# Experts' places as bfloat16 products, transposed feed-forwards and paired mLSTM heads in a two-block transformer kernel

## The chip, the cores and the metric

The kernel runs as one program on one core of a Trainium2 chip. The metric is the device time of one execution in microseconds (us); of several runs the median is given. Beside the times there is one execution recorded by the hardware profiler.

## The reference

Input is one sequence of 256 tokens by 1024 features in float32. Two blocks follow each other.

The first block adds two terms to x. One is attention: RMS norm, projection to q, k, v, four differential heads and eight plain heads, an output projection. The other is a mixture of 32 experts (four groups of eight): each token picks a group, then its two best experts in it, and `silu(t @ w_gate[e]) * (t @ w_up[e]) @ w_down[e]` of both is added with the router's weights.

The second block has four steps, each with its own RMS norm:

```python
x = x + 0.5 * swiglu(rms(x), w_gate, w_up, w_down)        # ffn1, hidden width 2816
z = rms(x) @ w_in + b_in                                  # split into q, k, v, conv inputs, gates
y_attn  = sliding_window_attention(a_q, a_k, a_v, sinks) @ w_proj_attn      # 16 heads, 4 kv heads, window 128
y_mlstm = (sigmoid(m_o) * rms(mlstm(m_q, m_k, m_v, m_i, m_f))) @ w_proj_mlstm  # 8 heads
x = x + (g0 * y_attn + g1 * y_mlstm) @ w_out              # this step is called mix below
x = x + 0.5 * swiglu(rms(x), ...)                         # ffn2, then a last RMS norm
```

## The kernel before

**Stages.** In order of time: attention of the first block (to about 141 us), experts (to about 341), ffn1 (to about 541), mix (to about 805) and ffn2 with the last norm.

**Dense products.** Float32 weights come as units of 128 x 1536 elements (768 KB) over SyncE's DMA queue (L104) into a ring of buffers. A unit is cut into pieces of 128 x 512, and each piece is split in two: ScalarE writes the rounded `hi` (L123), VectorE the rest `lo` (L132). Activations are split alike into `xh` and `xl`. Each product is then three TensorE passes (`mm3`: hi by xh, lo by xh, hi by xl), all issued by the helper `mm` (L207, in the changed kernel L220). There are two forms. `dense_tok` keeps 128 tokens stationary and streams 512 weight columns, so tokens end up on partitions. `dense_T` keeps a 128 x 128 piece of weights stationary and streams all 256 tokens, so features end up on partitions.

**Side work.** A `Side` object holds jobs (Python generators) that are advanced by `pump()`, which is called after each contraction step of a dense product; `yield 3` means three pumps later. TensorE and the other engines execute in the order in which the program issues, so the pumps fix where a small job's matmuls stand between the large ones.

**Feed-forward.** The hidden width 2816 is worked in 11 chunks of 256. For each chunk `dense_tok` makes gate and up side by side in two PSUM tiles (one for each half of the tokens), 48 matmuls of 512 columns. Then `hidden` runs as a side job: ScalarE takes silu of gate with the token's norm factor r as scale (L1297), VectorE multiplies by up and r (L1298), three pumps later TensorE transposes h in four small matmuls (L262), and h is split into `hh` and `hl` (L1304, L1305). The down product of the chunk before (24 matmuls) stands between one chunk's gate and up and the next's. r comes from GpSimd's Newton steps (L247 to L253).

**Experts.** Tokens are routed to 11 groups of four experts with 32 places each. P (256 tokens x 128 places, zeros and ones) is a group's placing matrix. The gather job collects x through P in two PSUM tiles of tag t, evacuated piece by piece by ScalarE (L1012) and VectorE (L1010) in turn; then two matmuls with P give the places' weights (`wsl`, L1022), and two transposes of P (L1025) the matrix PT for the way back. PSUM has two buffers of tag t and two of tag b.

**Mix.** For each of eight mLSTM heads a matmul with `pick` spreads the head's running maximum M over partitions (M holds 40 rows, L1410 and after), two matmuls make scores from 64 rows of q and k, and three more use them with the values. `window_job` does the window attention for two heads at a time, each with 64 rows of its own.

Of the kernel before, what the change touches and what calls it, by code (L numbers as in the profile page):

```python
# [10 lines left out]
F32 = mybir.dt.float32  # L11
# [8 lines left out]
D = 1024  # L20
# [27 lines left out]
class Stream:  # L48
# [31 lines left out]
    def early(self, first, pool, tag, bufs):  # L80

        self.open(pool, tag, bufs, self.k.stop)
        for i in range(first, first + bufs):
            self.fetch(i, self.pools[-1])
# [110 lines left out]

class Kernel:
# [68 lines left out]
    def new_xt(self):  # L265
        self.xt = (self.xp.tile([128, 8, S], F32R, name="xh", tag="xh"),
                   self.xp.tile([128, 8, S], F32R, name="xl", tag="xl"))
# [130 lines left out]
    def dense_T(self, acc, xt, cts=4, first=0):  # L398

        for kk in range(first, 8):  # L400
# [25 lines left out]
    def build(self):  # L426
# [29 lines left out]
        self.xn = self.xp.tile([128, 2, D], F32, name="xn")  # L456
# [29 lines left out]
    def qk_norm(self, at, acc, gcol, heads, name, then=None):  # L486
# [9 lines left out]
        if name == "qd":  # L496
            self.rB, self.rB2 = (at.tile([128, S], F32, name=f"rB{q}") for q in range(2))
# [6 lines left out]
        dst = heads[name] = at.tile([128, 4, S], F32, name=name, tag={"km": "qd"}.get(name, name))  # L504
# [163 lines left out]
    def attention1(self):  # L668
# [3 lines left out]
        with ExitStack() as es:  # L672
# [3 lines left out]
            self.new_xt()  # L676
            heads["y"] = y = self.xt
# [8 lines left out]
        y = [p[:, 4:] for p in y]  # L686
# [32 lines left out]
        self.st.open(self.xp, "xn", 1, self.stop)  # L719
        self.st.add_pool(self.xp, "xl", 1, self.last - 8)  # L720
# [10 lines left out]
    def diff_out(self, at, v, wT, heads):  # L731
# [5 lines left out]
        for h in range(4):  # L737
            p = self.pt([128, S], "b")
            c = slice(h * 128, (h + 1) * 128)
            self.mm(p, v[:, 0, c], wT[h][:, 0:256], True, False)  # L740
            self.mm(p[:, 128:256], v[:, 1, c], wT[h][:, 256:384], False, True)
# [20 lines left out]
    def moba_out(self, v, wT, y, j):  # L762
        nc = self.nc
        p = self.pt([128, S], "b")
        for hf in range(2):
# [3 lines left out]
            self.mm(p[o], v[:, 0, c], w[:, 0:256], True, False)  # L769
            self.mm(p[o, 128:256], v[:, 1, c], w[:, 256:384], False, True)  # L770
        nc.scalar.activation(y[0][:, 4 + j], p, AF.Copy)
        nc.vector.tensor_sub(y[1][:, 4 + j], p, y[0][:, 4 + j].bitcast(F32))

    def attention1_in(self, at):
# [41 lines left out]
        for n in range(2):  # L816
            acc = [self.pt([128, 512], "a") for tt in range(2)]
            self.dense_tok(acc, lambda kk: (xt[0], xt[1], kk))
            t = self.xn[:, n].rearrange("p (t n) -> p t n", t=2)
            nc.scalar.activation(t[:, 0], acc[0], AF.Copy, scale=self.r[:, 0:1])  # L820
            if n == 0:
                nc.scalar.activation(t[:, 1], acc[1], AF.Copy, scale=self.r[:, 1:2])
            else:
                nc.vector.tensor_scalar(t[:, 1], acc[1], self.r[:, 1:2], None, op0=OP.mult)
# [10 lines left out]
    def route_open(self):  # L835
# [6 lines left out]
        cb = bp.tile([128, 322], F32, name="cb")  # L842
        nc.scalar.dma_start(cb, self.i["cb"])
        self.iota, self.idx, self.e3 = (cb[:, a:b] for a, b in ((128, 256), (256, 289), (289, 322)))
        self.ones, self.before = (bp.tile([128, 128], BF16, name=f"m{q}") for q in range(2))
        nc.gpsimd.memset(self.ones, 1.0)
        nc.gpsimd.tensor_copy(self.before, cb[:, 0:128])
# [4 lines left out]
        self.le = [bp.tile([128, 4, 8], F32, name=f"le{tt}") for tt in two]  # L852
        self.oh = [[bp.tile([128, 33], BF16, name=f"oh{tt}{j}") for j in two] for tt in two]
        self.hT = self.xn.rearrange("p t (k n) -> p (t k) n", n=S)
# [38 lines left out]
    def select(self):  # L893
# [12 lines left out]
        key = bp.tile([128, 33], F32, name="key")  # L906
        km = bp.tile([128, NG], F32, name="km")
        self.eq = eq = bp.tile([128, NG, 3], F32, name="eq")
        pe = bp.tile([128, 2, NG, 3], F32, name="pe")
# [25 lines left out]
    def weigh(self):  # L935
# [46 lines left out]
        self.gov = bp.tile([128, 2, NG, 3], F32, name="gov")  # L982
# [305 lines left out]
    def hidden(self, fp, c, gu, hT, wait=False):  # L1288
# [4 lines left out]
        if c == 0 and wait:  # L1293
            yield 4
# [568 lines left out]
```

## Time and profile before

| | |
|---|---|
| time, median of 3 runs | 1005.68 us (1005.47 to 1006.81) |
| profiled execution | 1005.48 us, of which 1003.7 us are the span of the profile |
| TensorE busy | 986.8 us (98% of the span), granted clock at its upper level nearly throughout |
| VectorE, ScalarE, GpSimd busy | 560.8, 505.3, 50.3 us |
| DMA | 235.29 MB, 234 GB/s on average, above 410 GB/s in most of the expert stage |

A busy time is summed over an engine's instructions; the ends of matmuls are modelled, so the distance between two starts tells more about the price of a matmul than its listed duration. The chain of waits is followed back from the last instruction and says at each step what ended last.

### The profile page before, as it was taken

Reading aid. Unit: us, or ns where it says so; the run is one execution under the profiler, and the core shown is the slowest. Engines: PE = TensorE matmul, PEld = TensorE weight load, DVE = VectorE, ACT = ScalarE, POOL = GpSimd, SP = SyncE. Lnnn points to the kernel's source line nnn. Section 1 sums busy time; section 2 is a strip of 40 time slices with the busy share of each in tenths; the row PEclk is TensorE's granted clock in tenths of the full one; section 3 lists DMA queues with packets and bytes.
Section 4 is the critical chain, followed back from the end, with each engine's and each line's share of the span. In section 5 each row is a group of like instructions: output and inputs, shape, how many; then the busy total and the mean of one; then the engine's idle time right before and its main releaser. Section 6 shows DMA issues by size and latency. Waiting matters only on the chain.

```text
span 1003.7 us, 15460 instructions
## 1 busy us (share of the span) xinstructions
PE 986.8 (98%) x5690; PEld 735.0 (73%) x5690; DVE 560.8 (56%) x1261; ACT 505.3 (50%) x1080; POOL 50.3 (5%) x142
## 2 busy tenths in 40 slices
PE   8999999999999999999999999999999999999996
PEld 7977774444444478888888989776778888888885
DVE  4787753222222365455556795457886656555555
ACT  6767622122121365454556566556674565455554
POOL 2000200000000010000000200100200020000001
PEclk9999999999999999999999999999999999999999
DMA  9795699999999755546455554343444555555441
GB/s 336 300 381 182 222 362 392 415 416 415 416 417 412 321 183 188 196 160 208 167 188 185 178 197 163 133 156 126 146 155 166 189 205 189 189 174 193 169 146 42
DMA packets 47285, 235.29 MB, mean 234 GB/s; under 512 B 5425, under 2 KB 7757, under 8 KB 47208
## 3 DMA queue, kind: packets, MB, share of 16 engines
q1 hardware_dynamic: 45384, 229.94, 62.1%
q0 software_dynamic: 1248, 3.80, 1.4%
q8 instruction: 46, 0.75, 0.3%
q10 hardware_dynamic: 576, 0.55, 0.2%
q14 instruction: 31, 0.25, 0.1%
HBM read 233.20 MB, written 1.07 MB: 233 GB/s over the span
## 4 chain that ended last, share of the span: by engine, by line
PE 82%; DMA 11%; DVE 4%; ACT 2%; issue 1%; POOL 0%; POOLq 0%; SPq 0%; DVEq 0%; ACTq 0%
PE ps L207 79%; DMA unit<-in_wmo 10%; PE ps L262 1%; PE ps L288 1%; DMA unit<-in_wst 1%; DVE lo L132 1%; PE ps L1517 1%; ACT xg L1012 0%; DVE xg L1010 0%; DVE e L570 0%; PE ps L586 0%; DMA ident<-in_cg 0%; ACT e L571 0%; ACT hi L123 0%; PE ps L1025 0%
## 5 line engine op out<-in xcount | busy, mean ns | idle before, releaser
L132 DVE TENSOR_TENSOR lo<-unit,hi 128x512 fp32r<-128x512 f32 x480 | 315.7, 686 | 87.5 <-ACT hi L123 87.3
L123 ACT ACTIVATE hi<-unit 128x512 fp32r<-128x512 f32 x480 | 290.5, 627 | 137.1 <-PE ps L207 106.3
L207 PE MATMUL ps<-hi,xh 128*128 128x512 f32 (+1 forms) x576 | 232.2, 403 | 0.0
L207 PE MATMUL ps<-hi,xl 128*128 128x512 f32 (+1 forms) x576 | 226.4, 393 | 0.0
L207 PE MATMUL ps<-lo,xh 128*128 128x512 f32 (+1 forms) x576 | 226.3, 393 | 0.0
L207 PEld LDWEIGHTS ps<-hi,xh 128*128 128x128 f32 x576 | 108.4, 188 | 30.7 <-issue 6.0
L207 PEld LDWEIGHTS ps<-hi,xl 128*128 128x128 f32 x576 | 108.4, 188 | 25.6 <-DVE xl L293 0.2
L207 PEld LDWEIGHTS ps<-lo,xh 128*128 128x128 f32 x576 | 108.7, 189 | 22.7
L207 PE MATMUL ps<-unit,xg 128*32 x704 | 84.2, 598 | 0.0
L207 PE MATMUL ps<-xh,hi 128*128 128x256 f32 x272 | 78.0, 288 | 0.5 <-ACT hi L123 0.5
L207 PE MATMUL ps<-xh,lo 128*128 128x256 f32 x272 | 76.4, 283 | 1.0 <-DVE lo L132 1.0
L207 PE MATMUL ps<-xl,hi 128*128 128x256 f32 x272 | 76.0, 281 | 0.0
L207 PE MATMUL ps<-hi,hh 128*128 128x512 f32 (+1 forms) x178 | 71.9, 404 | 0.0
L207 PE MATMUL ps<-lo,hh 128*128 128x512 f32 (+1 forms) x178 | 70.0, 393 | 0.0
L207 PE MATMUL ps<-hi,hl 128*128 128x512 f32 (+1 forms) x178 | 69.9, 393 | 0.0
L1010 DVE TENSOR_SCALAR xg<-ps,pp 128x128 f32<-128x128 f32 x44 | 15.4, 351 | 75.5 <-ACT xg L1012 75.5
L1012 ACT ACTIVATE xg<-ps,pp 128x128 f32<-128x128 f32 x44 | 16.2, 367 | 79.4 <-PE ps L207 70.2
L207 PEld LDWEIGHTS ps<-xh,hi 128*128 128x128 f32 x272 | 51.0, 188 | 4.0 <-issue 2.2
L1298 DVE SCALAR_TENSOR_TENSOR h<-ps,r,s 128x256 f32<-128x256 f32 x44 | 20.9, 483 | 57.2 <-ACT s L1297 57.2
L207 PEld LDWEIGHTS ps<-xh,lo 128*128 128x128 f32 x272 | 50.8, 188 | 1.3 <-DVE lo L132 1.3
L207 PEld LDWEIGHTS ps<-xl,hi 128*128 128x128 f32 x272 | 51.2, 189 | 0.1
L207 PEld LDWEIGHTS ps<-P,x 128*128 128x128 f32 x352 | 41.5, 192 | 11.4 <-issue 7.3
(337 smaller groups left out, 1165.3 us busy)
## 6 DMA issues: line engine op xcount, KB each, us to landing
unit<-in_wst SPq DMA_DIRECT2D x158, 768.0 KB, 4.4
unit<-in_wmo SPq DMA_DIRECT2D x120, 768.0 KB, 14.7
unit<-in_wmo SPq DMA_DIRECT2D x12, 512.0 KB, 12.0
bb<-in_rows POOLq DMA_DIRECT2D x8, 256.0 KB, 4.1
nb<-toeplitz SPq DMA_DIRECT2D x6, 256.0 KB, 3.8
unit<-in_wst SPq DMA_DIRECT2D x3, 256.0 KB, 4.5
out<-o SPq DMA_DIRECT2D x3, 256.0 KB, 2.3
x<-in_x SPq DMA_DIRECT2D x2, 256.0 KB, 3.9
```

What stands on the lines that cost most here:

```text
L123: nc.scalar.activation(pair[0], src, AF.Copy)
L132: nc.vector.tensor_sub(pair[1], src, pair[0].bitcast(F32))
L207: self.nc.tensor.matmul(out, lhsT, rhs, start=start, stop=stop, skip_group_check=True)
L262: self.nc.tensor.transpose(p[:, j, tt * 128:(tt + 1) * 128], src[:, tt, (kk + j) * 128:(kk + j + 1) * 128], self.ident)
L288: nc.tensor.transpose(ps[j][:, tt * 128:(tt + 1) * 128], src[:, tt, (kk + j) * 128:(kk + j + 1) * 128], self.ident)
L1010: nc.vector.tensor_scalar(xg[:, kk + j], p[:, j], c, None, op0=OP.mult)
L1012: nc.scalar.activation(xg[:, kk + j], p[:, j], AF.Copy, scale=c)
L1298: nc.vector.scalar_tensor_tensor(h[:, tt], gu[tt][:, 256:512], r, s[:, tt], op0=OP.mult, op1=OP.mult)
L1517: nc.tensor.transpose(tp[:, b], e[hf][:, b * 128:(b + 1) * 128], self.ident)
```

## The change

1. **Feed-forwards transposed.** `ffn` calls `dense_T` instead of `dense_tok`, so h comes out with features on partitions, and `hidden` needs no transposes. r, which was a scale for each partition, is now spread over a tile `rF` by `spread_r` once in each feed-forward; VectorE multiplies gate by it, ScalarE takes silu, VectorE multiplies by up. Up is left without r; it comes back in the last step, where x takes the down product times `hr` = r/2 instead of 0.5.
2. **Experts.** P is copied to bfloat16 (`Pb`, GpSimd). The routing weights are cut in three bfloat16 parts (`gt3`), and the places' weights are the sum of three columns each. The ways back are two ordinary bfloat16 matmuls with an identity.
3. **mLSTM heads in pairs.** `M` and `pick` are made 128 rows high (zeros below). `mlstm_pair` handles two heads, with their score matmuls alternating between the upper and lower 64 rows. `window_job` issues its scores in the same alternating order, and its product with the values takes PSUM tag t instead of b.
4. **Split buffers.** xl is split into a tile of six and one of two slices (`Rows`), xn into three and one, so that freed parts can hold weights: two more expert units are fetched early, during attention, and several small tiles move into tags of others.

On TensorE, at the end of an expert group's gather (P or Pb with the group's routing weights, then the ways back), before:

```order
L207 MATMUL ps<-gtr,P 128x5 [waits DVE_49]
L207 MATMUL ps<-gtr,P 128x5
L1025 MATMUL ps<-ident,P 128x128 [waits DVE_49]
L1025 MATMUL ps<-ident,P 128x128
L207 ISA
```

and after:

```order
L220 LDWEIGHTS Pb [waits Pool_49]
L220 MATMUL ps<-gt_1941,Pb 128x15 [waits DVE_49]
L220 LDWEIGHTS Pb
L220 MATMUL ps<-gt_1941,Pb 128x15
L220 LDWEIGHTS Pb
L220 MATMUL ps<-identb,Pb 128x128 [waits DVE_49]
L220 LDWEIGHTS Pb
L220 MATMUL ps<-identb,Pb 128x128
L220 ISA
```

What was one instruction each (float32) is now a weight load and a matmul each, with 15 columns instead of 5, behind GpSimd's cast.

On TensorE in ffn1, second half of the contraction for chunks 0 and 1 (`hi`, `lo` weights, `xh`, `xl` and `xm` tokens, `h` the hidden values), before:

```order
L207 MATMUL ps<-hi,xh 128x512
L207 MATMUL ps<-lo,xh 128x512
L207 MATMUL ps<-hi,xl 128x512
L262 MATMUL ps<-ident,h 128x128 [waits DVE_49] x2
L262 MATMUL ps<-ident,h 128x128 x2
L207 MATMUL ps<-hi,xh 128x512 [waits Activation_49]
L207 MATMUL ps<-lo,xh 128x512 [waits DVE_49]
```

and after:

```order
L220 MATMUL ps<-xh,hi 128x256
L220 MATMUL ps<-xm,hi 128x256
L220 MATMUL ps<-xh,lo 128x256
L220 MATMUL ps<-ident,r 128x128 [waits PE_49,Pool_49]
L220 MATMUL ps<-ident,r 128x128
L220 MATMUL ps<-xh,hi 128x256 [waits Activation_49]
L220 MATMUL ps<-xl,hi 128x256
L220 MATMUL ps<-xh,lo 128x256 [waits DVE_49]
```

The transposes of h are gone, and the spreading of r (`ident,r`) now stands in the stream ahead of chunk 1's matmuls and waits for GpSimd (Pool).

On TensorE in mix, at the scores of one mLSTM head (`qk`), before:

```order
L207 MATMUL ps<-xl,hi 128x256
L207 MATMUL ps<-xh,lo 128x256
L207 MATMUL ps<-qk 128x256
L207 MATMUL ps<-qk 128x128
L207 MATMUL ps<-xh,hi 128x256 [waits Activation_49]
```

and of a pair, after:

```order
L220 MATMUL ps<-xl,hi 128x256
L220 MATMUL ps<-xh,lo 128x256
L220 MATMUL ps<-qk 128x256 x2
L220 MATMUL ps<-qk 128x128 x2
L220 MATMUL ps<-xh,hi 128x256 [waits Activation_49]
```

Two matmuls of one head in a row became four of two heads, alternating between them.

The diff, cut to its core:

```diff
-    def dense_T(self, acc, xt, cts=4, first=0):
-
-        for kk in range(first, 8):
+    def dense_T(self, acc, xt, cts=4, first=0, kks=range(8)):
+        for kk in kks[first:]:
...
+            self.st.early(NA + sum(RA), self.ra, "rawk", 1)
...
+            self.st.early(NA + sum(RA) + 1, self.xp, "xl", 1, self.last - 8)
...
+        self.gt3 = bp.tile([128, 2, NG, 3, 5], BF16, name="gt3")
+        rest = bp.tile([128, 2, NG, 5], F32, name="rest", tag="rt")
+        for n, t in enumerate((gtr, rest, rest)):
+            nc.vector.tensor_copy(self.gt3[:, :, :, n], t)
+            if n < 2:
+                nc.vector.tensor_tensor(rest, t, self.gt3[:, :, :, n], op=OP.subtract)
...
+        Pb = bp.tile([128, 2, 128], BF16, name="Pb")
+        nc.gpsimd.tensor_copy(Pb, P)
...
-        pw = self.pt([128, 5], "t")
+        pw = self.pt([128, 15], "t")
         for tt in range(2):
-            self.mm(pw, P[:, tt], self.gtr[:, tt, g], tt == 0, tt == 1)
+            self.mm(pw, Pb[:, tt], self.gt3[:, tt, g].rearrange("p n c -> p (n c)"), tt == 0, tt == 1)
         w = bp.tile([128, 2], F32, name="wsl", bufs=2)
+        parts = pw.rearrange("p (n c) -> p c n", n=3)
         for e in range(4):
             o = slice(CAP * e, CAP * e + CAP)
-            nc.vector.tensor_copy(w[o], pw[o, e:5:4 - e])
+            nc.vector.tensor_reduce(w[o], parts[o, e:5:4 - e], axis=AX.X, op=OP.add)
         pt = self.pt([128, S], "t")
         for tt in range(2):
-            nc.tensor.transpose(pt[:, tt * 128:(tt + 1) * 128], P[:, tt], self.ident)
+            self.mm(pt[:, tt * 128:(tt + 1) * 128], Pb[:, tt], self.identb, tt == 0, True)
...
-                gus = [[self.pt([128, 512], q) for tt in range(2)] for q in "ab"]
+                gus = [[self.pt([128, 2, S], q) for n in range(2)] for q in "ab"]
                 for half in range(2):
                     for c in range(2):
-                        self.dense_tok(gus[c], lambda kk: (xt[0], xt[1], kk), range(4 * half, 4 * half + 4))
+                        self.dense_T(gus[c], xt, kks=range(4 * half, 4 * half + 4))
...
-                    gu = [self.pt([128, 512], "b" if c else "a") for tt in range(2)]
-                    self.dense_tok(gu, lambda kk: (xt[0], xt[1], kk))
+                    gu = [self.pt([128, 2, S], "b" if c else "a") for n in range(2)]
+                    self.dense_T(gu, xt)
...
-                                self.x_add(tt, half, dn[tt][half], 0.5)
+                                self.x_add(tt, half, dn[tt][half], self.hr[:, tt:tt + 1])
...
-        s = fp.tile([128, 2, 256], F32, name="s", bufs=2)
-        h = fp.tile([128, 2, 256], F32, name="h", bufs=2)
-        if c == 0 and wait:
-            yield 4
-        for tt in range(2):
-            r = self.r[:, tt:tt + 1]
-            nc.scalar.activation(s[:, tt], gu[tt][:, 0:256], AF.Silu, scale=r)
-            nc.vector.scalar_tensor_tensor(h[:, tt], gu[tt][:, 256:512], r, s[:, tt], op0=OP.mult, op1=OP.mult)
-        yield 3
-        p = self.pt([128, 2, S], "t")
-        self.transposes(p, h, 0)
+        s = fp.tile([128, 2, S], F32, name="s", bufs=2)
+        if c == 0:
+            if wait:
+                yield 4
+            self.rF = fp.tile([128, S], F32, name="rF")
+            self.hr = fp.tile([128, 2], F32, name="hr")
+            nc.scalar.activation(self.rF, self.spread_r(), AF.Copy)
+            nc.gpsimd.tensor_scalar(self.hr, self.r, 0.5, None, op0=OP.mult)
+            yield 1
+        nc.vector.tensor_mul(s, gu[0], self.rF[:, None, :].to_broadcast([128, 2, S]))
+        nc.scalar.activation(s, s, AF.Silu)
+        yield 1
+        h = fp.tile([128, 2, S], F32, name="h", bufs=2)
         hh = fp.tile([128, 2, S], F32R, name="hh", bufs=2)
         hl = fp.tile([128, 2, S], F32R, name="hl", bufs=2)
-        nc.scalar.activation(hh, p, AF.Copy)
-        nc.vector.tensor_sub(hl, p, hh.bitcast(F32))
+        nc.vector.tensor_mul(h, gu[1], s)
+        nc.scalar.activation(hh, h, AF.Copy)
+        nc.vector.tensor_sub(hl, h, hh.bitcast(F32))
...
-        self.M = mx.tile([40, S], F32R, name="M2")
+        self.M = mx.tile([128, S], F32R, name="M2")
         nc.gpsimd.memset(self.M.bitcast(F32), 0.0)
-        self.pick = mx.tile([40, 8], F32R, name="pick")
-        nc.gpsimd.tensor_tensor(self.pick, self.ident[0:40, 0:8], self.ident[0:40, 32:40], op=OP.add)
+        self.pick = mx.tile([128, 8], F32R, name="pick")
+        nc.gpsimd.tensor_tensor(self.pick, self.ident[:, 0:8], self.ident[:, 32:40], op=OP.add)
...
-    def mlstm_head(self, mx, h, qk, mv, num, ssq):
...
-        pm = self.pt([128, S], "t")
-        self.mm(pm, self.pick[:, h:h + 1].to_broadcast([40, 128]), self.M)
...
-        q, k = qk[pr, h // 2], qk[pr, 4 + h // 2]
-        sc = self.pt([128, 384], "b")
-        self.mm(sc[:, 0:256], k[:, 0:128], q)
-        self.mm(sc[:, 256:384], k[:, 128:256], q[:, 128:256])
...
+    def mlstm_pair(self, mx, i, qk, mv, num, ssq):
+        nc = self.nc
+        two = range(2)
+        pm = self.pt([128, 2, S], "t")
+        E = [mx.tile([128, 384], F32, name="E", tag="e", bufs=6) for hf in two]
+        for hf in two:
+            h = 2 * i + hf
+            self.mm(pm[:, hf], self.pick[:, h:h + 1].to_broadcast([128, 128]), self.M, hf == 0)
...
+        yield 3
+        sc = [self.pt([128, 384], "b") for hf in two]
+        for c, k, q in ((slice(0, 256), slice(0, 128), slice(0, 256)),
+                        (slice(256, 384), slice(128, 256), slice(128, 256))):
+            for hf in two:
+                pr = slice(64 * hf, 64 * hf + 64)
+                self.mm(sc[hf][:, c], qk[pr, 4 + i, k], qk[pr, i, q])
+        for hf in two:
+            nc.vector.scalar_tensor_tensor(E[hf], sc[hf], 0.125, E[hf], op0=OP.mult, op1=OP.mult)
...
+        scs = [self.pt([128, 384], "b") for hf in range(2)]
+        for c, t, n in ((slice(0, 128), slice(0, 128), 128), (slice(128, 384), slice(128, 256), 256)):
+            for hf in range(2):
+                p = slice(64 * hf, 64 * hf + 64)
+                self.mm(scs[hf][:, c], aq[p, j, t], ak[p, jk, 0:n])
         for hf in range(2):
-            p = slice(64 * hf, 64 * hf + 64)
-            sc = self.pt([128, 384], "b")
-            self.mm(sc[:, 0:128], aq[p, j, 0:128], ak[p, jk, 0:128])
-            self.mm(sc[:, 128:384], aq[p, j, 128:256], ak[p, jk])
+            sc = scs[hf]
...
-            po = self.pt([128, 4, 128], "b")
+            po = self.pt([128, 4, 128], "t")
...
-                    self.side.add(*[self.mlstm_head(mx, h, qk, mv, num, ssq) for h in range(8)])
+                    for i in range(4):
+                        self.side.add(self.mlstm_pair(mx, i, qk, mv, num, ssq), iter(()))
```

## Rows read from the trace of the kernel before

**Rows 1.** The page: the chain that ended last, by line, shares of the span.

```profile
PE ps L207 79%; DMA unit<-in_wmo 10%; PE ps L262 1%; PE ps L288 1%; DMA unit<-in_wst 1%; DVE lo L132 1%; PE ps L1517 1%; ACT xg L1012 0%; DVE xg L1010 0%; DVE e L570 0%; PE ps L586 0%; DMA ident<-in_cg 0%; ACT e L571 0%; ACT hi L123 0%; PE 
```

**Rows 2.** Table by stage, 141 to 345 us; columns: busy (instructions) by engine, PEclk, DMA, GB/s.

```profile
141.00:345.00 204.00, 200.81 (x1573) 96.24 (x1573) 54.29 (x176) 44.47 (x104) 0.00 (x0) 1.00 1.01 409
```

**Rows 3.** TensorE's waits, 141 to 345 us (us in total, times, longest).

```profile
PE ps L207 <- ACT dh L1076: 0.7, 1, 0.7
```

**Rows 4.** The chain of waits, 379 to 400 us: start us, us, what.

```profile
379.09 16.86 PE ps L207 x72
395.95 0.44 PE ps L262 x4
```

**Rows 5.** TensorE's timeline, mix stage: start us, us, engine line op out<-in xcount.

```profile
569.56 0.28 PE L207 MATMUL ps<-xh,hi 128*128 128x256 f32 x1
...
581.07 0.40 PE L207 MATMUL ps<-hi,xh 128*128 128x512 f32 x1
```

**Rows 6.** Timelines of TensorE, GpSimd and ScalarE, ffn1's first chunks.

```profile
359.37 0.60 PE L288 MATMUL ps<-ident,x 128*128 128x128 f32 x4
...
369.93 0.20 POOL L253 TENSOR_TENSOR r<-r,nw_t 128x2 f32<-128x2 f32 x1
...
370.16 0.84 ACT L1297 ACTIVATE s<-ps,r 128x256 f32<-128x256 f32 x2 [3.54 <-POOL r L253]
```

**Rows 7.** Timelines of TensorE and GpSimd, ffn2's first chunk.

```profile
808.23 0.60 PE L288 MATMUL ps<-ident,x 128*128 128x128 f32 x4
...
820.25 0.19 POOL L253 TENSOR_TENSOR r<-r,nw_t 128x2 f32<-128x2 f32 x1
```

**Rows 8.** TensorE's timeline, the end of one group's gather.

```profile
241.42 0.61 PE L207 MATMUL ps<-gtr,P 128*128 128x5 f32 x4
242.12 0.44 PE L1025 MATMUL ps<-ident,P 128*128 128x128 f32 x2
242.49 0.64 PE L207 MATMUL ps<-unit,xg 128*32 x4
```

**Rows 9.** TensorE's timeline, bfloat16 products of the routing.

```profile
138.54 0.52 PE L207 MATMUL ps<-oh,m 128*128 128x33 bf16 x10
```

**Rows 10.** The chain of waits, a group's ways back.

```profile
223.27 0.36 DVE xg L1010
...
223.68 0.44 PE ps L1025 x2
```

**Rows 11.** TensorE's timeline around the spreading of one head's M.

```profile
616.91 0.28 PE L207 MATMUL ps<-xh,lo 128*128 128x256 f32 x1
617.13 0.38 PE L207 MATMUL ps<-M,pick 40*128 40x256 f32 x1
...
617.66 0.28 PE L207 MATMUL ps<-xl,hi 128*128 128x256 f32 x1
```

**Rows 12.** TensorE's timeline around one mLSTM head's scores.

```profile
620.29 0.28 PE L207 MATMUL ps<-xh,lo 128*128 128x256 f32 x1
620.51 0.92 PE L207 MATMUL ps<-qk 64*128 64x256 f32 x4
...
621.58 0.28 PE L207 MATMUL ps<-xl,hi 128*128 128x256 f32 x1
```

**Rows 13.** TensorE's timeline around the window scores of two heads.

```profile
667.63 0.40 PE L207 MATMUL ps<-hi,xl 128*128 128x512 f32 x1
667.96 0.93 PE L207 MATMUL ps<-ak,aq 64*128 64x128 f32 x8
...
669.16 0.40 PE L207 MATMUL ps<-lo,xh 128*128 128x512 f32 x1
```

**Rows 14.** TensorE's timeline, window scores (in brackets: idle before, and releaser).

```profile
701.78 0.92 PE L207 MATMUL ps<-ak,aq 64*128 64x128 f32 x4 [0.57 <-DVE yl L1534]
```

**Rows 15.** Timelines of TensorE and VectorE, the end of a chunk's gate and up.

```profile
391.35 0.39 PE L207 MATMUL ps<-hi,xl 128*128 128x512 f32 x1
...
392.28 0.48 DVE L1298 SCALAR_TENSOR_TENSOR h<-ps,r,s 128x256 f32<-128x256 f32 x1 [0.22 <-ACT s L1297]
```

More of the change, by code (lines that the diff above doesn't have):

```diff
@@ L78, in load_part, with early @@
         self.k.nc.sync.dma_start(self.tiles[0][0][:, c], self.units[0][0][:, c])
-    def early(self, first, pool, tag, bufs):
-        self.open(pool, tag, bufs, self.k.stop)
+    def early(self, first, pool, tag, bufs, stop=None):
+        self.open(pool, tag, bufs, stop or self.k.stop)
         for i in range(first, first + bufs):
@@ L193, in drain, with __init__, __getitem__ @@
             self.pump()
+class Rows:
+    def __init__(self, six, two):
+        self.tiles = six, two
+    def __getitem__(self, key):
+        p, k, *rest = key
+        span = isinstance(k, slice)
+        n = int((k.start if span else k) >= 6)
+        return self.tiles[n][(p, slice(k.start - 6 * n, k.stop - 6 * n) if span else k - 6 * n, *rest)]
 class Kernel:
@@ L266, in new_xt @@
         self.xt = (self.xp.tile([128, 8, S], F32R, name="xh", tag="xh"),
-                   self.xp.tile([128, 8, S], F32R, name="xl", tag="xl"))
+                   Rows(self.xp.tile([128, 6, S], F32R, name="xl", tag="xl"),
+                        self.xp.tile([128, 2, S], F32R, name="xm", tag="xm")))
     def to_xt(self, src, half, gain, tags="tt"):
@@ L455, in build @@
         nc.gpsimd.memset(self.eps, EPS)
-        self.xn = self.xp.tile([128, 2, D], F32, name="xn")
+        self.xn = [self.xp.tile([128, n, 512], F32, name=q) for q, n in (("xn", 3), ("xo", 1))]
         self.pp = con.tile([128, NPP], F32, name="pp")
@@ L496, in qk_norm @@
         if name == "qd":
-            self.rB, self.rB2 = (at.tile([128, S], F32, name=f"rB{q}") for q in range(2))
+            slot = self.ra.tile([128, 1536], F32, name="slot", tag="rawk")
+            heads["slot"], self.rB, self.rB2 = (slot[:, a:b] for a, b in ((0, 1024), (1024, 1280), (1280, 1536)))
             p = self.spread_r()
@@ L503, in qk_norm @@
         rts = yield from self.two_parts(at, rts, self.rB, self.halves)
-        dst = heads[name] = at.tile([128, 4, S], F32, name=name, tag={"km": "qd"}.get(name, name))
+        if name == "kd":
+            dst = heads[name] = heads["slot"].rearrange("p (c t) -> p c t", c=4)
+        else:
+            dst = heads[name] = at.tile([128, 4, S], F32, name=name, tag={"km": "qd"}.get(name, name))
+        if name == "km":
+            self.st.early(NA + sum(RA), self.ra, "rawk", 1)
         for h in range(2):
@@ L675, in attention1 @@
             acc = [[self.pt([128, 512], "a") for tt in range(2)] for n in range(2)]
-            self.new_xt()
-            heads["y"] = y = self.xt
+            y = self.xp.tile([128, 8, S], F32R, name="y", tag="xh")
+            heads["y"] = y = y[:, 0:4], y[:, 4:8]
+            self.st.early(NA + sum(RA) + 1, self.xp, "xl", 1, self.last - 8)
             self.out1(acc, heads["yd"], 0, 0)
@@ L851, in route_open @@
         self.mk = [bp.tile([128, 4], F32, name=f"mk{tt}") for tt in two]
-        self.le = [bp.tile([128, 4, 8], F32, name=f"le{tt}") for tt in two]
+        self.le = [bp.tile([128, 4, 8], F32, name=f"le{tt}", tag=("eq", "le1")[tt]) for tt in two]
         self.oh = [[bp.tile([128, 33], BF16, name=f"oh{tt}{j}") for j in two] for tt in two]
-        self.hT = self.xn.rearrange("p t (k n) -> p (t k) n", n=S)
+        self.hT = Rows(*(t.rearrange("p t (k n) -> p (t k) n", n=S) for t in self.xn))
         self.P = {}
@@ L981, in weigh @@
         nc.vector.tensor_copy(self.cmi, cm)
-        self.gov = bp.tile([128, 2, NG, 3], F32, name="gov")
+        self.gov = bp.tile([128, 2, NG, 3], F32, name="gov", tag="gov")
         nc.vector.tensor_scalar(tmp, self.eq, 1.0 * CAP, CAP - 1000.0, op0=OP.mult, op1=OP.add)
@@ L1073, in parts @@
     def parts(self):
-        self.ds = dh, dl = [self.bp.tile([128, 512], F32R, name=n) for n in ("dh", "dl")]
+        self.ds = dh, dl = [self.xp.tile([128, 512], F32R, name=n, tag=t) for n, t in (("dh", "xm"), ("dl", "xo"))]
         self.nc.scalar.activation(dh, self.dn, AF.Copy)
```

83 lines of the change are left out of this document (43 added, 40 removed).

## The prediction

> **What bounds the kernel now.** I read the chain of waits first. It names matmuls for 79% of the span and, as its only other large line, the landing of expert weights (`unit<-in_wmo`) for 10% [rows 1]. Those DMA pieces lie in the expert stage, 141 to 345 us, so the second view is the table of that stage [rows 2]: TensorE is busy 200.81 of 204 us, and the DMA engines are full as well (share 1.01, 409 GB/s). Two resources are full, and the chain can name only one. The list of TensorE's waits in that stage decides: its longest line is 0.7 us, for `dh`, and no line of it names a weight unit [rows 3]. TensorE sets the time there, and weights land ahead of it. The other stages are plainer: in ffn1 the chain is nothing but matmuls and small transposes [rows 4]. So every part of the change is to be priced by what it takes off TensorE's in-order stream, and by the new waits that it puts into it.
>
> Durations come from the profiled execution, 1005.48 us (span 1003.7 and 1.78 outside it, taken as unchanged). It lies 0.20 under the median of the runs, 1005.68.
>
> **Feed-forwards.** One chunk is 72 matmuls of 512 columns, 16.86 us, and four transposes of h, 0.44 us [rows 4]. A 512-column matmul is thus 16.86/72 = 234.2 ns, and the 48 of gate and up are 11.24 us. The change makes them 96 matmuls of 256 columns with the weights stationary. This form stands in the trace: 96 of them run from 569.56 to 581.07 in the mix stage [rows 5], 11.51 us, or 119.9 ns each. So gate and up lose 0.27 us a chunk, the transposes give 0.44 back: -0.17 us, by 11 chunks in each feed-forward -1.9 us, for both -3.7 us. Bounds: +0.27 x 22 = +5.9 us if the transposes' time came back in another way, and -0.44 x 22 = -9.7 us if the narrower form cost nothing.
>
> The Trainium skill (TensorE: Matmul & The Clock Gate, "Back-to-back issue gap") gives a spacing of N/2.4 + 2.5 ns: 109.2 ns for 256 columns and 215.8 for 512, so halving would cost only 2.6 ns a pair. The trace has 234.2 and 119.9 [rows 4, 5], 5.6 ns a pair; an estimate by the page would make the feed-forwards 48 x 22 x 3 ns = 3 us cheaper. The measurement decides here.
>
> Since tokens now lie along the free axis, r (the norm's factor per token) must be spread over partitions: `spread_r`, four small matmuls in each feed-forward, about the 0.44 us of four transposes in rows 4, and 0.5 us with the copy's hand-over: +0.5 for each.
>
> The new wait is on r. In ffn1, ScalarE waits 3.54 us for r, which GpSimd finishes at 369.93 + 0.20 = 370.13 [rows 6]; TensorE does not wait, as the r-scaled work is only in the evacuation. After the change the spread matmuls stand in TensorE's queue behind the second chunk half, 72 matmuls after the last transposes of x (they start at 359.37, 0.44 us). TensorE is there at 359.81 + 72 x 0.1199 = 368.44, and everything behind it waits until 370.13: **+1.7 us** (0 if r comes earlier because ScalarE's squares do; 3 if the copy's latency adds to it). In ffn2 r is ready at 820.44 [rows 7], and 120 matmuls of 256 columns lie between the transposes (808.23 + 0.44) and the spread: 808.67 + 14.39 = 823.06. There 2.6 us of cover remain, and I cost the wait at nothing; if r came 3 us later it would cost 0.4.
>
> Sum: ffn1 -1.9 + 0.5 + 1.7 = +0.3; ffn2 -1.9 + 0.5 = -1.4.
>
> **Experts.** The places' matrix P becomes bfloat16; weights (three bfloat16 parts, 15 columns) and ways back (transposes) use it. The two weight matmuls and their passes are 241.42 to 242.12, the transposes 242.12 to 242.49 [rows 8], 0.70 + 0.37 us a group. A bfloat16 product is far cheaper: ten of 33 columns have a busy time of 0.52 us [rows 9]. But the transposes' result takes the PSUM buffer of the second gathered half, and that is emptied by evacuations that alternate between ScalarE and VectorE. The chain of waits passes through them in the groups before 225 us: VectorE's `xg` from 223.27 for 0.36 us, and the transposes at 223.68, right behind its end at 223.63 [rows 10]. No part of the change touches these evacuations, so cheaper weight matmuls turn into a wait for the same `xg`, and only the transposes get shorter, 0.37 to some 0.2: -0.15 a group over ten groups. Bounds: 0 (if GpSimd's cast Pb came late) and -0.8 a group or -8 us (if the wait did not hold). I take -1.5, since the chain shows the evacuation as what ends last.
>
> The two extra weight units, loaded early in attention, move 2 x 768 KB out of the full DMA stage: 1.9 us each at 409 GB/s. With no unit among TensorE's waits they are worth nothing. Their new place: attention's DMA queue has room; bounds there are 0 and +3.8 us if both held up a unit in need. I take 0. GpSimd casts and five VectorE instructions of `gt3` lie beside TensorE work.
>
> **Mix.** The matmul that spreads a head's M over partitions has 40 rows. One stands with two plain matmuls between the starts at 616.91 and 617.66 [rows 11]: 0.75 us for the three, less two of 0.12, so it costs 0.51. With 128 rows it is an ordinary 256-column matmul, 0.12: -0.39 x 8 = **-3.1 us** (0 if the price isn't one of the shape).
>
> The scores of one head (64 rows) take 620.29 to 621.58 less two plain ones, 1.29 - 0.24 = 1.05 us [rows 12]. Paired, upper and lower half of the array work together. The window attention's scores do this already for two heads: 667.63 to 669.16 less two of 0.234, 1.53 - 0.47 = 1.06 us for twice the columns [rows 13]. So 8 x 1.05 becomes 4 x 1.06: **-4.2 us** (bounds 0 and, with no cost at the seams, -6).
>
> Pairs and single heads go at the same pace per head, so ScalarE and GpSimd have the same work in the same time; a pair late by 1 us at its `mv,E` products would cost 4 us over four pairs. The buffer moved from tag b to t removes at best the one wait of 0.57 us for `yl` [rows 14]: -0.4. The reordered window scores get 0. Mix: -7.7.
>
> **Sum:** -1.5 + 0.3 - 1.4 - 7.7 = -10.3, and 1005.48 - 10.3 = **995.2 us**.
>
> **Rivals.**
> 1. The evacuations are not what holds the ways back, and all of the bfloat16 saving comes out: -8 instead of -1.5, 988.7 us. For it: TensorE's list has hardly a wait for `xg`. Against: the weight matmuls now fill that time, and the chain passes through `xg` all the same [rows 10].
> 2. The chain is right that DMA sets the expert stage. Then two units ahead give -3.8 and the bfloat16 parts nothing: 992.9. Against: the list of waits [rows 3].
> 3. Pairs don't overlap in the order written (upper and lower head alternately, two PSUM tiles), so the 4.2 goes: 999.4.
> 4. The reordering of window scores gains too, as alternating halves overlap better than both products of one half in a row: 8 jobs, at most half of 1.06 each, -4.2: 991.0. By the Trainium skill (TensorE: Matmul & The Clock Gate, on row and column tiles) a weight load passes a running matmul only where the row group differs, and matmuls start in order, which speaks for it. Against it speaks [rows 12, 13]: twice the columns at the same time means that the old order overlaps already.
> 5. **Slower.** The feed-forward's elementwise chain grows: VectorE multiplies by r, ScalarE does silu, and one pump later VectorE multiplies by up. That last step frees the PSUM pair that the next chunk's gate and up need, 24 matmuls (5.6 us) later; six matmuls in (0.7 us), the second tile is needed. Before, the last matmul of a chunk starts at 391.35 and h is done at 392.28 + 0.48 [rows 15], 1.2 us after it ends. After, three operations of about 0.7, a pump of 1.4 and two splits of 0.7 queued ahead are 4.9, under 6.3. If splits queue deeper, each us past 6.3 costs 1 us in each of 20 chunks: from 0.5 us on, the gain of 10.3 is gone; at 0.6, 1007.2.
> 6. It does not do what it says: the price of the 40 and 64 rows stays in new shapes, and the stall in ffn1 grows to 3. Then only -1.5 and -0.1 and -0.4 remain: some 1003.5 to 1005.
>
> **How the numbers follow.** The forecast 0.60, its own range 991.5 to 999 (the pieces' bounds taken singly); rival 1: 0.11; 2: 0.05; 3: 0.10; 4: 0.05; 5: 0.05; 6: 0.04. Range 989.5 to 1000.5: outside lie rivals 1, 5 and 6. What can be told from no change begins at 0.2%, 2 us: faster 0.92, same 0.03, slower 0.05.
>
> **What would show it.** In the profile after: chunks of feed-forward at 17.13 us; a wait of TensorE for r in ffn1 of 1.7 us and none in ffn2; in the expert stage a new wait of about 0.5 us a group before the ways back, on VectorE's or ScalarE's `xg`; the pick matmul spaced 0.12; paired scores at 1.06 for two heads. A TensorE wait on `h` in each chunk would show rival 5, and groups shorter by 0.8 us instead of 0.15 would show rival 1. The forecast is wrong if the mix stage does not shorten by 6 us or more.

## The result and the profile after

The changed kernel takes 993.75 us (median of 4 runs, 993.68 to 993.92) against 1005.63 us before (1005.47 to 1006.81): -11.9 us, ratio 0.988 with a 95% interval of 0.9862 to 0.9897. The forecast was 995.2 us with a range of 989.5 to 1000.5. The profiled executions have spans of 1003.7 and 992.1 us. They are divided here by TensorE's marks, in us from the start: the first matmul through P (141.17 before, 141.46 after), a group of transposes of x at the start of ffn1 (340.56, 338.98), of mix (540.26, 539.34) and of ffn2 (808.23, 799.00), and the start of the last matmul. All stages named below, of experiments too, are cut at these marks.

| stage | before, us | after, us | difference | forecast |
|---|---|---|---|---|
| attention, to the first gather | 141.17 | 141.46 | +0.3 | 0 |
| experts | 199.39 | 197.52 | -1.9 | -1.5 |
| ffn1 | 199.70 | 200.36 | +0.7 | +0.3 |
| mix | 267.97 | 259.66 | -8.3 | -7.7 |
| ffn2, to its last matmul | 187.64 | 185.04 | -2.6 | -1.4 |
| rest | 7.81 | 8.04 | +0.2 | 0 |

**Experts.** The table of the stage over the same window, to be read against [rows 2]: TensorE's busy time fell from 200.81 to 196.17 us, while the DMA share stayed full.

```profile
141.00:345.00 204.00, 196.17 (x1566) 92.69 (x1567) 55.62 (x182) 45.06 (x105) 4.69 (x13) 1.00 1.00 404
```

TensorE's waits in that window (us in total, times, longest) say where the difference between less work and less time is. Ten waits of 0.5 us for `xg` stand there now:

```profile
PE ps L220 <- DVE xg L1043: 5.0, 10, 0.6
PE ps L220 <- ACT dh L1110: 0.7, 1, 0.7
...
PE ps L220 <- POOL Pb L1033: 0.6, 1, 0.6
```

The list of before has a single wait of 0.2 us for `xg`, ahead of the ways back:

```profile
PE ps L1025 <- DVE xg L1010: 0.2, 1, 0.2
```

The end of one group's gather in the timelines of TensorE and VectorE shows it in place (in brackets the idle time before, and its releaser). It answers to [rows 8, 10]: the weight matmuls end early, the ways back start when VectorE's `xg` ends.

```profile
240.65 0.21 PE L220 MATMUL ps<-gt,Pb 128*128 128x15 bf16 x2
241.35 0.27 PE L220 MATMUL ps<-identb,Pb 128*128 128x128 bf16 x2 [0.49 <-DVE xg L1043]
241.55 1.06 PE L220 MATMUL ps<-unit,xg 128*32 x8
...
240.94 0.35 DVE L1043 TENSOR_SCALAR xg<-ps,pp 128x128 f32<-128x128 f32 x1 [0.43 <-ACT xg L1045]
```

From 241.35 the ways back take 0.20 us where they took 0.37. The weight matmuls and the wait of 0.49 together take 0.70 us (240.65 to 241.35), as the float32 weight matmuls alone did before: what they saved became the wait. From group to group the ways back stand 18.28 us apart (18.45 before). No wait on `unit<-in_wmo` is listed.

**Feed-forwards.** A chunk in the timeline, from one down product to the next (`hi,hh` at its start, `xh,hi` the first matmul of gate and up), answers to [rows 4, 5]. It is 409.98 - 392.89 = 17.09 us in ffn1, of which 11.52 are the 96 narrow matmuls and 5.57 the down product.

```profile
392.89 0.39 PE L220 MATMUL ps<-hi,hh 128*128 128x512 f32 x1
...
398.46 0.28 PE L220 MATMUL ps<-xh,hi 128*128 128x256 f32 x1
...
409.98 0.39 PE L220 MATMUL ps<-hi,hh 128*128 128x512 f32 x1
...
837.06 0.40 PE L220 MATMUL ps<-hi,hh 128*128 128x512 f32 x1
...
854.08 0.39 PE L220 MATMUL ps<-hi,hh 128*128 128x512 f32 x1
```

In ffn2 it is 854.08 - 837.06 = 17.02. The wait on r in ffn1, forecast at 1.7 us [rows 6], is there with 1.92 us:

```profile
369.50 0.71 PE L220 MATMUL ps<-ident,r 128*128 128x128 f32 x4 [1.92 <-POOL r L266]
```

**Mix.** Timeline of TensorE around one pair's pick and its scores, against [rows 11, 12]:

```profile
616.08 0.28 PE L220 MATMUL ps<-xh,lo 128*128 128x256 f32 x1
616.20 0.39 PE L220 MATMUL ps<-M,pick 128*128 128x256 f32 x2
616.43 0.28 PE L220 MATMUL ps<-xh,hi 128*128 128x256 f32 x1
...
620.62 0.28 PE L220 MATMUL ps<-xh,lo 128*128 128x256 f32 x1
620.82 0.92 PE L220 MATMUL ps<-qk 64*128 64x256 f32 x8
...
621.90 0.28 PE L220 MATMUL ps<-xl,hi 128*128 128x256 f32 x1
```

Two picks take 616.43 - 616.20 = 0.23 us, 0.12 each, where one took 0.51. Two heads' scores take 621.90 - 620.62 less two plain matmuls, 1.28 - 0.24 = 1.04 us, where one head's took 1.05.

### The profile page after: what moved, and what is told of

It reads as the page before. It is cut to its first block, busy times and chain, and to the rows that moved or that the text cites. A ratio compares the mean times of both kernels' runs of the same rounds, so it can differ in the third digit from the quotient of the medians.

```text
span 992.1 us, 17501 instructions
## 1 busy us (share of the span) xinstructions
PE 968.9 (98%) x6644; PEld 773.7 (78%) x6644; DVE 570.8 (58%) x1266; ACT 494.5 (50%) x1060; POOL 55.0 (6%) x156
## 4 chain that ended last, share of the span: by engine, by line
PE 63%; DVE 1%; POOL 1%; ACT 1%; issue 0%; POOLq 0%; DVEq 0%; ACTq 0%
PE ps L220 62%; PE ps L302 1%; PE ps L1568 1%; ACT xh L306 0%; DVE xl L307 0%; PE ps L275 0%; DVE x L316 0%; POOL nw_t L260 0%; ACT junk L325 0%; DVE lo L132 0%; DVE late L1766 0%; ACT hi L123 0%; POOL nw_t L265 0%; POOL nw_t L261 0%; POOL r L266 0%
## 5 line engine op out<-in xcount | busy, mean ns | idle before, releaser
L220 PE MATMUL ps<-xh,hi 128*128 128x256 f32 x976 | 276.5, 284 | 0.2 <-ACT hi L123 0.2
L220 PE MATMUL ps<-xh,lo 128*128 128x256 f32 x976 | 275.3, 283 | 1.1 <-DVE lo L132 1.1
L220 PE MATMUL ps<-xl,hi 128*128 128x256 f32 x732 | 205.6, 282 | 0.1
L220 PEld LDWEIGHTS ps<-xh,hi 128*128 128x128 f32 x976 | 183.8, 189 | 5.0 <-issue 3.0
L220 PEld LDWEIGHTS ps<-xh,lo 128*128 128x128 f32 x976 | 182.8, 187 | 1.3 <-DVE lo L132 1.3
L220 PEld LDWEIGHTS ps<-xl,hi 128*128 128x128 f32 x732 | 138.0, 189 | 1.4 <-DVE xl L307 0.3
L220 PE MATMUL ps<-hi,xh 128*128 128x512 f32 (+1 forms) x208 | 83.9, 403 | 0.0
L220 PE MATMUL ps<-lo,xh 128*128 128x512 f32 (+1 forms) x208 | 80.5, 387 | 0.0
L220 PE MATMUL ps<-hi,xl 128*128 128x512 f32 (+1 forms) x156 | 60.4, 387 | 0.0
L220 PEld LDWEIGHTS ps<-hi,xh 128*128 128x128 f32 x208 | 39.1, 188 | 12.8 <-issue 4.6
```

The lines of the kernel that those rows point to most:

```text
L220: self.nc.tensor.matmul(out, lhsT, rhs, start=start, stop=stop, skip_group_check=True)
```

## The experiments

All are the changed kernel with one edit, unless said otherwise; longer edits are cut to their core (`...`). Each time stands beside the time of the kernel before, run in turn with it on the same chip. The intervals of the ratios are about 1.7 us wide to either side, and a fall of TensorE's granted clock, told under e3, lengthens single executions by 1 to 2 us. Differences of that size between two versions therefore rest on the stages of the profiled executions, one of each version, and not on the times.

**e1: heads one by one.** `mlstm_head` from before, with the 128-row pick.

```diff
...
-                    for i in range(4):
-                        self.side.add(self.mlstm_pair(mx, i, qk, mv, num, ssq), iter(()))
+                    self.side.add(*[self.mlstm_head(mx, h, qk, mv, num, ssq) for h in range(8)])
```

> The changed kernel (993.75 us) with the mLSTM heads one by one again, the 128-row pick kept. Theory: two heads' scores cost in the trace after what one head's cost before (1.04 against 1.05 us), so four times 1.05 come back: 997.9 us. Rival: the pairs only shift work between pumps and the gain of the mix stage comes from the pick and the values' buffer: within 0.5 us of 993.75.

999.18 us (before: 1006.28), ratio 0.9929 [0.9913, 0.9946], 7.1 us under the kernel before, where the change is 11.9 under it: 4.8 us came back. In its profile mix is 4.1 us longer than after the change, and the other stages agree within 0.1. The pairs are worth what the theory said.

**e2: pick of 40 rows.**

```diff
-        self.M = mx.tile([128, S], F32R, name="M2")
+        self.M = mx.tile([40, S], F32R, name="M2")
...
```

> The changed kernel with M and pick 40 rows high again, pairs kept. Theory: a matmul of 40 rows between matmuls of 128 rows costs 0.39 us more than one of 128. Two of them now stand side by side, so the price of the change of shape is paid once a pair if it lies in the change (4 x 0.39 = +1.6, 995.3 us), or for each if it lies in the matmul itself (8 x 0.39 = +3.1, 996.9 us). Rival: the rows don't matter, 993.75.

996.59 us (before: 1006.28), ratio 0.9898 [0.9882, 0.9915]; mix is 1.5 us longer than after the change. The profiled execution (997.02 us) loses another 1.5 us in ffn1, where nothing is edited (see e3); by the time alone the other branch of the expectation would seem to hold. The timeline:

```profile
617.53 0.28 PE L220 MATMUL ps<-xh,lo 128*128 128x256 f32 x1
617.74 0.49 PE L220 MATMUL ps<-M,pick 40*128 40x256 f32 x2
...
618.39 0.28 PE L220 MATMUL ps<-xl,hi 128*128 128x256 f32 x1
```

From 617.53 to 618.39 are two picks and two plain matmuls, 0.86 - 0.24 = 0.62 us, 0.39 more than for two picks of 128 rows. A single one cost 0.39 more before. So the price is paid once for the neighbours, at the change of shape, not for each matmul, and four pairs at 0.39 are the 1.5 us of the stage. The Trainium skill (TensorEngine Tiling (Array Packing), Key Properties) says that changing the tiling mode drains the array. The trace fits that, with 0.39 us for the change, if 40 rows make another mode than 128, which no run shows directly. The 3.1 us of the prediction are right as a sum, since before every pick stood alone; with pairs and 40 rows half of it would have been saved anyway.

**e3: the values' product in tag b.**

```diff
-            po = self.pt([128, 4, 128], "t")
+            po = self.pt([128, 4, 128], "b")
```

> The changed kernel with the window's product with the values in PSUM tag b again. The prediction gave this part 0.4 us; the chain of waits of before and after differs by 1.5 us at this place (10.12 us between two groups of transposes against 8.64). If the wait for yl is all: 994.2 to 994.3 us. If the two heads of the next scores are also torn apart by the wait and pay for two single heads: +1.5, 995.2 us.

995.12 us (before: 1006.28), ratio 0.9887 [0.987, 0.9903]; mix is 1.3 us longer. The prediction gave this part 0.4. The timeline after the change, where the eight score matmuls of the next job stand together behind the values' product, and the next dense matmul follows 693.15 - 692.29 = 0.86 us after the first of them:

```profile
692.29 0.93 PE L220 MATMUL ps<-ak,aq 64*128 64x128 f32 x8
693.15 0.50 PE L220 MATMUL ps<-hi,xh 128*128 128x512 f32 x1
```

and of e3, where the buffers of tag b come free one after the other:

```profile
693.92 0.49 PE L220 MATMUL ps<-ak,aq 64*128 64x128 f32 x2
695.41 0.92 PE L220 MATMUL ps<-ak,aq 64*128 64x128 f32 x6 [1.01 <-DVE yl L1585]
696.26 0.50 PE L220 MATMUL ps<-hi,xh 128*128 128x512 f32 x1
```

The job starts with one product of one head alone (two matmuls of the record, 0.48 us), waits 1.01 us, and goes on at 695.41: 2.34 us from its start to the next dense matmul. The six matmuls behind the wait take 0.85 us to it, as long as all eight after the change (0.86). So of the 1.48 us more, 1.01 are the listed wait, and the other 0.47 are the product ahead of it, which overlapped with nothing. Before, the row with the wait of 0.57 us [rows 14] held one head's four matmuls alone, and the other head's four stood ahead of the wait.

In ffn1 this execution is 1.5 us longer than that of the changed kernel, though nothing is edited there. The table of stretches with TensorE's granted clock (after the instruction counts of POOL) shows why, in e3:

```profile
368.00:370.00 2.00, 0.38 (x3) 0.39 (x4) 0.00 (x0) 0.00 (x0) 1.39 (x7) 1.00 1.01 332
...
371.00:372.00 1.00, 1.00 (x7) 1.00 (x6) 1.00 (x2) 0.76 (x2) 0.00 (x0) 0.50 0.25 104
...
373.00:374.00 1.00, 1.00 (x7) 1.00 (x6) 0.44 (x1) 1.00 (x2) 0.00 (x0) 0.50 0.00 0
...
375.00:376.00 1.00, 1.00 (x11) 1.00 (x10) 0.45 (x1) 0.31 (x1) 0.00 (x0) 1.00 0.32 59
```

and in the changed kernel:

```profile
368.00:370.00 2.00, 0.50 (x5) 0.51 (x5) 0.00 (x0) 0.00 (x0) 1.27 (x7) 1.00 1.03 237
...
371.00:372.00 1.00, 1.00 (x11) 1.00 (x10) 0.95 (x2) 0.76 (x3) 0.00 (x0) 1.00 0.41 172
```

Both waited 1.92 us for r. Behind the wait the clock was granted at half (0.50, the 1.2 GHz level) from 371 to 374 us in e3, and at full speed in the other. e2 and e4 show the same 1.5 us and the same fall. Of the eight profiled executions with this wait of 1.9 us (the changed kernel's, e1 to e4, e6, e7 and e9) these three show the fall; of the five with a shorter wait or none at this place (e5, e8, e10 to e12) none does. So the wait seems to have a second price that some executions pay. That it brings the fall on is read from its place right behind the wait; what decides between the executions is not shown, and e6 and e12 have such a fall in other places.

**e4: window scores in the old order.**

```diff
-        for c, t, n in ((slice(0, 128), slice(0, 128), 128), (slice(128, 384), slice(128, 256), 256)):
-            for hf in range(2):
+        for hf in range(2):
+            for c, t, n in ((slice(0, 128), slice(0, 128), 128), (slice(128, 384), slice(128, 256), 256)):
```

> The changed kernel with the window scores in the old order (both products of one head, then both of the other). Theory: they overlap in either order, as rows 13 of before showed: 993.75 within 0.3 us. Rival 4 of the prediction: alternating halves gain, so the old order costs up to 0.5 us for each of 8 jobs, 994.8 to 998 us.

994.88 us (before: 1006.28), ratio 0.9884 [0.9868, 0.9901]; mix differs by 0.06 us, the rest is ffn1's clock. The reordering by itself is worth nothing, and rival 4 falls. The rule of the Trainium skill that it quotes (TensorE: Matmul & The Clock Gate, on row and column tiles) speaks for an alternating order. No run here shows a gain of that order for 64-row matmuls.

**e5: feed-forwards as before.** `ffn` and `hidden` of the kernel before, and 0.5 for `hr` in the last step.

> The changed kernel with both feed-forwards as before (tokens stationary, transposes of h, no spreading of r). By the stages of the two traces ffn1 lost 0.2 us and ffn2 won 2.5 us, so 996.0 us; by the prediction's own terms (ffn1 +0.3, ffn2 -1.4) 994.9. The wait for r on TensorE goes. Rival: the shorter chunks come from something else than the form (the granted clock, DMA), then they stay and the time falls by the 1.9 us of the wait, 991.9.

995.35 us (before: 1005.94), ratio 0.9891 [0.9875, 0.9908]. ffn1 is 0.7 us shorter than after the change, ffn2 2.6 us longer, chunks are at 17.30 and 17.28 us again. In sum transposing is worth 2 us, and in ffn1 it costs.

**e6: places' weights in float32.**

```diff
-            self.mm(pw, Pb[:, tt], self.gt3[:, tt, g].rearrange("p n c -> p (n c)"), tt == 0, tt == 1)
+            self.mm(pw, P[:, tt], self.gtr[:, tt, g], tt == 0, tt == 1)
...
```

> The changed kernel with the places' weights as float32 products again (5 columns, four copies), the ways back still bfloat16. Theory: the weight matmuls fill time in which TensorE waits for xg anyway (5.0 us over ten groups in the trace after); so 993.75 within 0.5 us, and the waits for xg in the list fall from 5.0 us to near 0. Rival 1: their time counts, 0.5 us in each of ten groups, 998.5 us.

994.97 us (before: 1005.94), ratio 0.9886 [0.987, 0.9903]. In the profile the expert stage is 197.76 us (197.52 after the change); its list has no wait for `xg`, and the ways back start behind the longer weight matmuls at the same distance as before:

```profile
243.05 0.61 PE L220 MATMUL ps<-gtr,P 128*128 128x5 f32 x4
243.75 0.27 PE L220 MATMUL ps<-identb,Pb 128*128 128x128 bf16 x2
```

(243.05 to 243.75 are 0.70, as 240.65 to 241.35 after the change.) The execution is longer elsewhere: attention by 2.2 us, with a granted clock of 0.59 from 12 to 16 us. The weights in bfloat16 by themselves are worth 0.2 us of the 5 that their shorter matmuls give, and rival 1 falls.

**e7: one evacuation for each gathered tile.**

```diff
...
-                if j % 2:
-                    nc.vector.tensor_scalar(xg[:, kk + j], p[:, j], c, None, op0=OP.mult)
-                else:
-                    nc.scalar.activation(xg[:, kk + j], p[:, j], AF.Copy, scale=c)
...
+            nc.vector.tensor_mul(xg[:, kk:kk + 4], p, c[:, :, None].to_broadcast([128, 4, 128]))
```

> The changed kernel with each gathered PSUM tile emptied by one VectorE multiplication of 128 x 512 (gains broadcast) in place of four alternating ones. The four take 1.56 us, one should take about 0.7, as the 128 x 512 splits from SBUF do. Theory: the wait of 0.5 us for xg before the ways back goes in each of ten groups, 988.8 us, DMA still ahead. Rival: with groups 0.5 us shorter the expert stage reaches the DMA engines' pace, full at 409 GB/s; then at most 1 to 2 us of the 5 come out, 992 us, and TensorE's list of waits names unit<-in_wmo.

987.75 us (before: 1005.94), ratio 0.9817 [0.9801, 0.9834]: 6 us less than the change. The timeline has one VectorE instruction of 0.69 us in the place of four in a chain of 1.53 us (239.76 to 241.29), and no wait ahead of the ways back:

```profile
236.74 0.69 DVE L1041 TENSOR_TENSOR xg<-ps,pp 128x512 f32<-128x512 f32 x1 [2.29 <-PE ps L220]
...
237.63 0.21 PE L220 MATMUL ps<-gt,Pb 128*128 128x15 bf16 x2
237.70 0.27 PE L220 MATMUL ps<-identb,Pb 128*128 128x128 bf16 x2
```

Groups are 17.64 us apart, 0.64 less. TensorE now waits once for a weight unit, 0.6 us:

```profile
PE ps L220 <- ACT dh L1106: 0.7, 1, 0.7
PE ps L220 <- DMA unit<-in_wmo: 0.6, 1, 0.6
```

**e8: r spread one pump later in ffn1.**

```diff
-            if wait:
-                yield 4
+            yield 4 if wait else 1
```

> The changed kernel with the spreading of r in ffn1 one pump (12 matmuls, 1.44 us) later. Theory: TensorE's wait for r falls from 1.9 to about 0.5 us, and the chain to the first down product has enough room, so 992.4 us. Rival: the chain from r through silu and h to the first down product is what ends last, and the time moves there: 993.7, with a new wait for hh or hl.

992.69 us (before: 1005.94), ratio 0.987 [0.9853, 0.9886]. The wait for r fell to 0.81 us (0.5 was expected), ffn1 by 1.1, and the clock stayed full behind the wait. The chain to the first down product did not become the bound.

**e9: two units not early.**

```diff
...
-            self.st.early(NA + sum(RA), self.ra, "rawk", 1)
...
-            self.st.early(NA + sum(RA) + 1, self.xp, "xl", 1, self.last - 8)
...
+        self.st.open(self.ra, "rawk", 1, self.stop)
+        self.st.add_pool(self.xp, "xl", 1, self.last - 8)
```

> The changed kernel with the two additional expert units no longer fetched early in attention, but opened with the other buffers after it (same number of buffers). Theory of the prediction: weights lie ahead of TensorE with room, so nothing changes, 993.75 within 0.5 us (0.7 us at most, from the split that stands ahead of the last addition to x on VectorE). Rival 2: the DMA engines set the expert stage, then 2 x 1.9 us come back, 997.5 us.

994.05 us (before: 1006.11), ratio 0.9885 [0.9869, 0.9902]; the expert stage is 197.52 us, the same. Rival 2 falls, though the DMA engines are full throughout: what counts is whether a unit lands before its use.

**e10: e7 and e8 together.**

> Both gains together: gathered tiles emptied by one VectorE multiplication each, and r spread one pump later in ffn1. Theory: independent, -5.6 us and -1.1 us by the stages of the two traces, 993.75 - 6.7 = 987.0 us. Rival: the expert stage's end is now set by the last weight units, so the second gain is unchanged but the first varies with DMA, 987 to 988 us.

986.72 us (985.77 to 987.78; before: 1006.11), ratio 0.9811 [0.9795, 0.9828]. The gains add up in the stages: experts 6.2 us and ffn1 1.1 us shorter than after the change. The median is the lowest of the versions tried, 7 us under the change, but the intervals of e7, e11 and e12 overlap with this one.

**e11: e10 without early units.**

> As the kernel with both gains, but the two additional expert units not early. In the trace of the one-multiplication kernel TensorE waits 0.6 us for unit<-in_wmo, so weights are hardly ahead any more. Theory: now the early units are worth their transfer, 2 x 1.9 us less the room that is left: 987 + 2 to 4 = 989 to 991 us, with waits on in_wmo in TensorE's list. Rival: still room, 987 us.

987.90 us (before: 1006.11), ratio 0.9819 [0.9803, 0.9835]. The expert stage is 0.8 us longer than in e10, with one wait of 0.6 us for a unit. But e7 and e12, which have the early units, wait for a unit as well (0.6 and 0.4 us), and e7's stage is only 0.2 us shorter than this one. The 2 to 4 us expected did not come, and that the early units are worth anything here is not shown.

**e12: e10 with two pumps.**

> As the kernel with both gains, but r spread two pumps later in ffn1. Theory: no wait for r is left (0.8 us with one pump), but h is then made in the last pump ahead of the first down product and TensorE waits there for hh or hl about 2 to 3 us: 988.5 to 989.5 us. Rival: the chain still fits, 986.3 us.

987.87 us (985.70 to 988.57; before: 1006.11), ratio 0.9812 [0.9796, 0.9828], not to be told from e10. The expectation was wrong: r is no longer waited for, and the first down product waits only 0.38 us for `hh`:

```profile
366.19 0.61 PE L220 MATMUL ps<-ident,r 128*128 128x128 f32 x4
...
370.05 0.50 PE L220 MATMUL ps<-hi,hh 128*128 128x512 f32 x1 [0.38 <-ACT hh L1337]
```

In its profile ffn1, from the second group of transposes of x on (352.37 us; 349.52 in e10), is 0.2 us shorter than in e10. By the marks of the table it is 0.7 us longer, as the granted clock fell to half from 334 to 337 us. In the table by stretch the clock stands behind GpSimd's count, 0.72 on average:

```profile
332.00:336.00 4.00, 3.30 (x14) 2.64 (x15) 2.92 (x7) 1.86 (x5) 0.00 (x0) 0.72 1.02 416
```

Ahead of this fall TensorE was idle for 0.7 us and less at a time, at the end of the expert stage. e10 has the same short waits there and keeps the full clock.

## Why the prediction was right

**Which resource sets the expert stage** was read rightly from the list of waits against the chain: DMA pieces made 10% of the chain, and two transfers fewer changed nothing (e9). After the change TensorE's list names no unit either, though the DMA share of the stage is 1.00.

**Places in bfloat16.** -0.17 a group was measured, -0.15 forecast; the remainder of the saving turned into the forecast wait on `xg` (5.0 us over ten groups), and e6 and e7 show it from both sides: putting the cost back costs 0.2 us, shortening the evacuation brings 5.6 us in the stage. The stage fell by 1.9, not 1.5. The difference lies between the first two ways back: 168.33 - 154.28 = 14.05 us before, 168.20 - 154.57 = 13.63 after and 13.90 in e6, so there about half of the 0.49 us saved on the weights came out. From then on the distances are 18.45 and 18.28.

**Feed-forwards.** The sign and the mechanism held; the size of a chunk was off. -0.17 us was forecast for each, -0.21 and -0.27 were measured. The term that was mis-sized is the down product, which the working left out as unchanged: after the change its 24 matmuls take 5.57 us in ffn1 and 5.50 in ffn2 (820.03 to 825.53), 232 and 229 ns each, where they took 234. The narrow matmuls cost 120 ns as forecast. e5 shows that the old spacing returns with the old form. Why the same matmuls are closer together between narrow ones, and closer in ffn2, is open. Of ffn2's 2.6 us, 1.2 were not forecast. ffn1 came out 0.4 us dearer than forecast all the same: the stretch from its mark to the last transposes of x is 358.34 - 338.98 = 19.36 us, where it was 359.37 - 340.56 = 18.81 before and is 18.81 again in e5. What makes it longer, beside the narrower form that the working counts, is open.

**The wait on r** was forecast at 1.7 and measured at 1.92 us, in ffn1 alone, and ffn2 has none. What no row of before could show is the halved clock behind it in some executions (e3).

**Mix.** Pick and pairs: 606.93 to 676.42 before became 606.10 to 668.43, which is -7.2 us against -3.1 - 4.2 = -7.3 forecast. e1 confirms 4.1 for the pairs; e2 confirms the price of the shape and corrects where it is paid. The change of tag was taken for 0.4 and is worth 1.3 (e3): the row of 0.57 us was the idle time only, and the lost overlap of the two heads around it was not counted; from one group of transposes of e to the next there are 704.30 - 694.18 = 10.12 us at this place before, 694.81 - 686.17 = 8.64 after, and 10.12 again in e3. This is the second term that was too small.

**Rivals.** 1 fell by e6, 2 by e9, 3 by the trace and e1, 4 by e4. Rival 5 did not come: TensorE's list has no wait for h, silu or a PSUM pair in any chunk. Neither did rival 6: the picks are at 0.12 us, the pairs at 1.04, the wait on r at 1.92 and not 3. (By the prediction's own numbers a wait of 3 would make the feed-forwards +0.2, not the -0.1 in its sum.)

**The number.** By stages the spans differ from the forecast by -0.4 us in the experts, +0.4 in ffn1, -0.6 in mix, -1.2 in ffn2 and +0.5 in attention and the rest, together -1.3. The two terms that were too small, ffn2 and the tag, were partly cancelled by ffn1 and by the stages that the forecast put at nothing: misses of 2.2 us one way and 0.9 the other. That the total came out this near is in part luck.

## What to carry to other kernels

A full DMA queue in the chain of waits is not yet a bound: look whether the engine that uses the data ever waits for it. When work is made cheaper ahead of a fixed release, find that release first; here a chain of four small evacuations was worth three times what the cheaper matmuls were. Where two matmuls of half the array's height overlap, a wait between them can cost the overlap as well as its idle time: here 1.48 us for a wait of 1.01.

## What the runs showed of the hardware

- After an idle time of 1.92 us between busy stretches the granted clock fell to 0.50 for about 3 us in three profiled executions and stayed at 1.00 in five others with the same wait; with 0.8 us in the same place (e8, e10, e11) none of the three shows a fall. In e12 the clock fell to 0.50 at the end of the expert stage, where no single wait is over 0.7 us. So the length of one wait does not decide it by itself.
- A 40-row matmul among 128-row ones costs 0.39 us more [rows 11], two side by side cost the same 0.39 together (e2).
- The 512-column matmul is spaced 234 ns in long rows and 229 to 232 ns in groups of 24 between narrow ones.
- One VectorE evacuation of 128 x 512 from PSUM with a broadcast factor takes 0.69 us; four of 128 x 128, alternating between two engines that wait for each other, take 1.53.
